# Three weights' splitting moved into the first up projection and kept in DRAM, memory row sums taken from token rows, memory softmax scaling moved to ScalarE

## Chip, cores and metric

The kernel runs on one core of one Trainium2 chip. The metric is the device time of one execution in microseconds (us). Before the change it is 2209.2 us, the median of three runs (2208.19 to 2209.79).

## What is computed

One layer of a decoder trunk over 1024 tokens of width 1024, all in float32:

```
x = x + 1/2 * SwiGLU_1(RMSNorm(x))                 # D_FF = 2816
h = RMSNorm(x); z = h @ W_in                       # [u | v | c_q | c_kv | k_rope | q_mem | gates]
A: u * (tril(W_s) LayerNorm(v) + b)                # 128-token chunks, 8 groups of 64
B: multi-head latent attention, causal, 8 heads
C: cross-attention of q_mem into 256 memory tokens, 4 heads of 128:
   kv = RMSNorm(mem) @ w_kv; k = RMSNorm(k); p = softmax(q k^T / sqrt(128)); p @ v
merged = sum_i sigmoid(gate_i) * (y_i @ W_branch_i)
x = x + merged @ W_out
x = x + 1/2 * SwiGLU_2(RMSNorm(x))
```

The outputs are compared in float32, so each product is made of three matmuls in the faster format fp32r. A number is taken apart into a high part "hi" (its cast to fp32r) and a low part "lo" (what the cast left over), and hi·hi, lo·hi and hi·lo are added.

## The kernel before

**Products and splits.** A product is emitted by a helper whose three matmuls have the lines L147, L148 and L149. A weight, in a load of 512 KB (128 partitions of 1024 numbers), is split by `split`: a cast on ScalarE (ACT, L130) writes `whi`, and a subtraction on VectorE (DVE, L131) writes `wlo`. `split_later` does the same on L135 and L136. The pools decide what may run ahead: `whi` and `wlo` have five tiles each, `raw` three, `w4` eleven, `x4` ten.

**The up projection.** Each feed-forward network is worked off in "units", one for each block f of 128 gate and 128 up columns. A unit makes seven products instead of eight (a Strassen-like scheme), each of 12 matmuls over 512 tokens: 84 matmuls a unit. It needs four pairs of split weights, in this order: "a" (whole 128x1024), "s", "t" (128x1024, sums of loaded halves, made on DVE at L1321) and "l" (128x512). The results of the products are combined on DVE (`add`, L1348), go through a silu on ACT (L1600) and are multiplied by the gate on DVE (L1596). The first product of a unit multiplies by `a`, into the accumulator called `bank`; the last five go into accumulators called `one` or `bank`. Behind each odd f, `spill` subtracts the blocks of two units from each other (on POOL, L1750) and SP stores seven blocks to DRAM (L1757: `tdb` for blocks of the result, `tdt` for their differences).

`up(4)` runs the units f = 4 to 21. In it TensorE's (PE) order is as written in the program. The order on ACT, DVE, POOL and SP (SyncE, which issues nearly all DMAs) is set when the kernel is built, by a scheduler that weighs readiness against the order in the program. On the chip every engine works off its own list strictly in order, and so does SP: an instruction that waits holds all that stand behind it.

**The mixer.** Between the two feed-forward networks stand the input projection, the gates, and the mixer. In the mixer, `sgu` (branch A) loads `w_v` by `load`: pieces of 512 KB into `raw`, each split in halves of 512 columns by L130 and L131 right before the products that use them. `take(0)` and `take(1)` make the v projection of two groups of tokens, `mix` the chunked gating (its u is written by ACT at L662). Beside them the memory side (branch C) goes step by step: `mem_norm` squares the transposed memory on ACT, adds the squares on DVE and sums them over partitions on PE (`token_sums`); `mem_kv` loads the two halves of `w_kv` by `load` and makes keys and values; `mem_attention` makes the softmax: a maximum on DVE (L818), eight exponentials with sums on ACT (L823, 128x256 each) for two tiles, and a multiplication by the reciprocal sums on DVE (L828, 128x1024, eight in all).

## Time and profile before

| what | value |
|---|---|
| median of three runs | 2209.2 us |
| the profiled execution's own time | 2208.74 us |
| its span, first to last instruction | 2206.9 us |
| mean granted TensorE clock in it | 0.996 |
| HBM read / written | 206.00 MB / 86.51 MB |
| up projection, f = 4 to 21 | about 75 to 440 us of the span |
| mixer with memory attention | about 1075 to 1235 us of the span |

The time of an execution is 1.8 us more than its span. Times in the profile are in microseconds from the span's start. A row of the timeline has start, duration, engine, line, operation, output<-inputs and shapes; in brackets how long the engine was idle before it, and what released it. PE's matmuls are pipelined: in full flow one of 128x512 starts every 0.227 us (84 of them make a unit of 19.05 us), though each is shown with 0.39 us. "SPq" is the issue of a DMA by SP; the landing comes later.

### The profile page before, as it was taken

The page shows a single profiled execution, that of the slowest core. Times are in us where ns is not written, and L with a number is a line of the kernel's source. Part 1 is how long each engine was busy: PE and PEld are TensorE (multiplying, and loading weights), DVE is VectorE, ACT ScalarE, POOL GpSimd, SP SyncE. Part 2 cuts the span into 40 slices and gives each one's busy share as a digit, 9 for nine tenths or more (in the row PEclk, how much of TensorE's full clock was granted, in tenths as well). Part 3 has the DMA queues.
Part 4 walks back from the last instruction along what each step waited for, and adds up shares of the span by engine and source line. Part 5 has one row for each costly group of instructions (what it writes and reads, how often), then busy time and mean ns, then how long its engine had stood idle before and what let it go on. Part 6 is the DMA issues. An engine that isn't in the chain of part 4 may idle for free.

```text
span 2206.9 us, 27578 instructions
## 1 busy us (share of the span) xinstructions
PE 2177.5 (99%) x10256; PEld 1816.0 (82%) x10256; DVE 1564.4 (71%) x2402; ACT 912.1 (41%) x1507; POOL 249.4 (11%) x252
## 2 busy tenths in 40 slices
PE   9999999999999999999989999999999999999999
PEld 5788888888887888888878889988888888888887
DVE  7966666579889555544887669885886666657884
ACT  5422222244445333344465449843432222234332
POOL 0012111100000000000400121150011121210000
PEclk9999999999999999999999999999999999999999
DMA  4242323484432333331644740084032333338543
GB/s 144 82 153 91 102 99 110 144 309 157 148 107 93 117 105 124 134 103 39 220 134 148 255 170 30 30 315 181 29 120 97 101 113 100 115 110 300 172 129 105
DMA packets 116085, 294.29 MB, mean 133 GB/s; under 512 B 13680, under 2 KB 22000, under 8 KB 115952
## 3 DMA queue, kind: packets, MB, share of 16 engines
q1 hardware_dynamic: 115952, 292.55, 38.1%
q8 instruction: 80, 1.31, 0.2%
q14 instruction: 53, 0.43, 0.1%
HBM read 206.00 MB, written 86.51 MB: 133 GB/s over the span
## 4 chain that ended last, share of the span: by engine, by line
PE 88%; DVE 7%; ACT 2%; DMA 1%; issue 1%; SPq 0%; POOL 0%; ACTq 0%; DVEq 0%; POOLq 0%
PE one L147 14%; PE one L148 14%; PE one L149 14%; PE bank L147 13%; PE bank L148 12%; PE bank L149 12%; PE mm L147 1%; PE mm L148 1%; PE mm L149 1%; PE bank L948 1%; PE bank L963 1%; PE bank L964 1%; DVE wlo L136 1%; DVE wlo L131 1%; PE bank L425 1%
## 5 line engine op out<-in xcount | busy, mean ns | idle before, releaser
L135 ACT CAST whi<-x 128x1024 fp32r<-128x1024 f32 (+1 forms) x201 | 191.2, 954 | 501.6 <-PE one L148 220.5
L1348 DVE TENSOR_TENSOR t<-t,one 128x512 f32<-128x512 f32 x186 | 127.7, 687 | 244.1 <-PE one L149 243.3
L147 PE MATMUL bank<-h,whi 128*128 128x512 f32 x676 | 263.3, 390 | 0.0
L148 PE MATMUL bank<-h,whi 128*128 128x512 f32 x676 | 263.1, 389 | 0.0
L149 PE MATMUL bank<-h,wlo 128*128 128x512 f32 x676 | 263.0, 389 | 0.0
L136 DVE TENSOR_TENSOR wlo<-x,whi 128x1024 fp32r<-128x1024 f32 (+1 forms) x201 | 239.8, 1195 | 31.7 <-ACT whi L135 31.6
L147 PE MATMUL one<-h,whi 128*128 128x512 f32 x508 | 198.7, 391 | 0.7 <-ACT t L1457 0.7
L149 PE MATMUL one<-h,wlo 128*128 128x512 f32 x508 | 197.7, 389 | 0.0
L148 PE MATMUL one<-h,whi 128*128 128x512 f32 x508 | 197.6, 389 | 0.0
L147 PE MATMUL one<-w,whi 128*128 128x512 f32 x424 | 164.9, 389 | 0.0
L148 PE MATMUL one<-w,whi 128*128 128x512 f32 x424 | 164.9, 389 | 0.0
L149 PE MATMUL one<-w,wlo 128*128 128x512 f32 x424 | 164.9, 389 | 0.0
L130 ACT CAST whi<-w 128x1024 fp32r<-128x1024 f32 (+1 forms) x108 | 95.1, 899 | 144.6 <-PE one L148 62.7
L1750 POOL TENSOR_TENSOR raw<-raw 128x512 f32<-128x512 f32 x38 | 62.9, 1656 | 804.0 <-DVE raw L1596 804.0
L131 DVE TENSOR_TENSOR wlo<-w,whi 128x1024 fp32r<-128x1024 f32 (+1 forms) x108 | 110.2, 1034 | 60.6 <-ACT whi L130 60.5
L149 PEld LDWEIGHTS bank<-h,wlo 128*128 128x128 f32 x676 | 126.9, 188 | 26.3
L148 PEld LDWEIGHTS bank<-h,whi 128*128 128x128 f32 x676 | 126.9, 188 | 26.2
L147 PEld LDWEIGHTS bank<-h,whi 128*128 128x128 f32 x676 | 126.9, 188 | 26.1
L147 PE MATMUL bank<-whi 128*128 128x512 f32 x352 | 136.9, 389 | 0.0
L148 PE MATMUL bank<-wlo,whi 128*128 128x512 f32 x352 | 136.9, 389 | 0.0
L149 PE MATMUL bank<-whi,wlo 128*128 128x512 f32 x352 | 136.9, 389 | 0.0
L147 PEld LDWEIGHTS one<-h,whi 128*128 128x128 f32 x508 | 95.4, 188 | 20.9 <-ACT t L1457 1.1
(398 smaller groups left out, 4893.9 us busy)
## 6 DMA issues: line engine op xcount, KB each, us to landing
x<-in_ffn_w_gu_dram SPq DMA_DIRECT2D x78, 512.0 KB, 4.9
w<-tdt SPq DMA_DIRECT2D x40, 512.0 KB, 4.4
tdb<-raw SPq DMA_DIRECT2D x64, 256.0 KB, 2.1
h<-in_ffn_w_down_dram SPq DMA_DIRECT2D x64, 256.0 KB, 6.0
gate<-raw SPq DMA_DIRECT2D x31, 512.0 KB, 2.6
w<-tdb SPq DMA_DIRECT2D x30, 512.0 KB, 4.6
tdt<-w SPq DMA_DIRECT2D x48, 256.0 KB, 2.0
x<-in_w_gate_dram SPq DMA_DIRECT2D x21, 512.0 KB, 5.6
```

The source lines that it names most:

```text
L130: self.nc.scalar.copy(hi, src)
L131: return (eng or self.nc.vector).tensor_tensor(lo, src, hi.bitcast(F32), op=ALU.subtract)
L135: self.nc.scalar.copy(hi, src)
L136: return lambda: self.nc.vector.tensor_tensor(lo, src, hi.bitcast(F32), op=ALU.subtract)
L147: i = mmul(out, s[0], m[0], start=first, stop=False, **kw)
L148: mmul(out, s[0], m[1], start=False, stop=False, **kw)
L149: self.last = mmul(out, s[1], m[0], start=False, stop=last, **kw)
L425: nc.tensor.transpose(b[:m, k * P:(k + 1) * P], s, self.ident)
L948: nc.tensor.transpose(b[:, at:at + P], prs[t][:, kk * P:(kk + 1) * P], self.ident)
L963: nc.tensor.matmul(o, w, pt[0], start=n == 0, stop=False)
L1348: return self.nc.vector.tensor_tensor(out, x, y, op=ALU.add)
L1750: sub = lambda d, x, y: (eng or nc.gpsimd).tensor_tensor(d, x, y, op=ALU.subtract)
```

## The change

Four edits.

1. A generator `pre_split` is given to `up(4)` as `aside` and takes one step behind each unit from f = 4 on. A step loads 512 KB of `w_v` (four pieces), of the memory keys' weights (four) or of the memory values' weights (four) into a tile of `w4`, splits it by `split`, and stores `whi` and `wlo`, 512 KB each, to DRAM. Twelve units, f = 4 to 15, have such a step. In `sgu` and `mem_kv`, `load_parts` fetches the split pairs straight into `whi` and `wlo`, with no splitting.
2. `mem_norm` gets the sums of squares of the memory's tokens from their rows: two more loads of 512 KB (a new input, the same numbers in another layout, made beforehand like the other layouts), and two squares on ACT that add along the row. The squares of the transposed memory, the additions on DVE and the sum over partitions on PE go.
3. In the softmax of the memory attention, the multiplication by the reciprocal sum is done by ACT, four of 128x256 for each tile, instead of one of 128x1024 on DVE.
4. In `sgu`, the loads of the layer norm's rows go into a tile of `x4`; `next(mem)` moves out of `take(0)`; the memory queries' first step comes behind `mix(1)`'s second, followed by three steps of `branches`; the memory attention's list loses three such steps.

```diff
 
     def __init__(self, ctx, tc, a, out):
         self.tc, self.nc, self.a, self.out, self.last = tc, tc.nc, a, out, None
+        self.parts = {}
         pool = lambda name, bufs=1, **k: ctx.enter_context(tc.tile_pool(name=name, bufs=bufs, **k))
         self.const = pool("const")
         self.small = pool("small", 4)
...
                 self.split(hi[:, c], lo[:, c], raw[:, c], self.nc.gpsimd if at in pool else None)
                 at += 1
             out += [(hi[:, k * width:(k + 1) * width], lo[:, k * width:(k + 1) * width]) for k in range(m)]
+        return out
+
+    def pre_split(self, srcs, room):
+
+        nc = self.nc
+        for key, src in srcs:
+            n, width = src.shape[1:]
+            per = D // width
+            self.parts[key] = parts = [
+                [self.dram.tile([P, D], F32, name=f"pre_{key}_{k}_{x}") for x in "hl"] for k in range(n // per)]
+            for k, part in enumerate(parts):
+                raw = room().rearrange("p a w -> p (a w)")
+                nc.sync.dma_start(raw, src[:, k * per:(k + 1) * per, :].rearrange("p k w -> p (k w)"))
+                hi, lo = self.wide("whi"), self.wide("wlo")
+                self.split(hi, lo, raw)
+                for d, x in zip(part, (hi, lo)):
+                    nc.sync.dma_start(d, x.bitcast(F32))
+                yield
+
+    def load_parts(self, key, width):
+
+        out = []
+        for part in self.parts.pop(key):
+            pair = self.wide("whi"), self.wide("wlo")
+            for x, d in zip(pair, part):
+                self.nc.sync.dma_start(x.bitcast(F32), d)
+            out += [tuple(x[:, k:k + width] for x in pair) for k in range(0, D, width)]
         return out
 
     def mm(self):
...
         nc, a, tc = self.nc, self.a, self.tc
         v8 = lambda tag, dt=F32R: p.tile([P, 4, SGW], dt, name=tag, tag=tag, bufs=2)
         if True:
-            ln_g = self.bcast_row(p, "ln_g", a["sg_ln_g"], SGW)
-            ln_b = self.bcast_row(p, "ln_b", a["sg_ln_b"], SGW)
+            ln = self.x4()
+            ln_g, ln_b = (ln[:, k] for k in range(2))
+            for x, n in ((ln_g, "sg_ln_g"), (ln_b, "sg_ln_b")):
+                nc.sync.dma_start(x, a[n].partition_broadcast(P))
             ws = self.raw().rearrange("p (g t) -> p g t", g=SGG)
             nc.sync.dma_start(ws, a["sg_w"])
             nc.gpsimd.affine_select(
...
             self.split(whi, wlo, ws)
             mem = self.mem_norm()
             next(mem)
-            w = self.load(a["w_v"])
+            w = self.load_parts("v", SGW)
             next(mem)
             vs, yt = [], []
 
...
                     nc.vector.tensor_tensor(u, u, b, op=ALU.mult)
                     self.split(*(t[:, hf * 512:hf * 512 + 512] for t in yt[j]), u)
 
-            take(0, {7: lambda: next(mem)})
+            take(0)
             take(1, {3: lambda: next(mem)})
             m0, m1 = mix(0), mix(1)
             with tc.manual_schedule(engines={mybir.EngineType.PE}):
                 kv = self.mem_kv(next(mem), (lambda: next(m0, None), lambda: next(m0, None)))
                 rooms = [v8(n).rearrange("p (a b) w -> p a (b w)", a=2) for n in ("v_hi", "v_lo")]
                 queries = self.mem_queries([(x[:, 0], x[:, 1]) for x in rooms])
-                next(queries)
                 next(m1)
                 rooms = [v8(n, F32) for n in ("v_hi", "v_lo")]
                 rooms = [x.rearrange("p (a h) (b m) -> p a (h b) m", a=2, b=2)[:, k] for x in rooms for k in range(2)]
                 branch = self.branches(0, yt, sink)
                 next(branch)
                 next(m1, None)
+                next(queries)
+                for _ in range(3):
+                    next(branch)
             yc = self.mem_attention(next(queries), rooms, *kv, branch)
         return yc
 
...
             nc.sync.dma_start(
                 t.rearrange("p a (b m) -> p (a b) m", b=2), a["mem"][:, 4 * n:4 * n + 4])
         yield
-        acc = self.row()[:, :2 * ML].rearrange("p (a m) -> p a m", a=2)
-        for n, t in enumerate(x4):
-            sq = self.x4() if n == 0 else sq2
-            nc.scalar.activation(sq, t, ACT.Square)
-            if n == 0:
-                first, sq2 = sq, self.x4()
-        nc.vector.tensor_tensor(first, first, sq2, op=ALU.add)
-        nc.vector.tensor_tensor(acc, first[:, 0].rearrange("p (a m) -> p a m", a=2),
-                                first[:, 1].rearrange("p (a m) -> p a m", a=2), op=ALU.add)
-        nc.vector.tensor_tensor(acc[:, 0], acc[:, 0], acc[:, 1], op=ALU.add)
+        ss = self.stat("mem_ss", ML // P)
+        sq = self.x4(BF16)
+        for t in range(ML // P):
+            row = self.x4()
+            nc.sync.dma_start(row.rearrange("p a w -> p (a w)"), a["mem_rows"][t])
+            nc.scalar.activation(sq, row, ACT.Square, accum_out=ss[:, t:t + 1])
+        r = self.rms(ss, ML // P, D)
         yield
-        ss = self.token_sums(acc[:, 0], late=True)
-        last = self.final
-        r = self.rms(ss, ML // P, D)
-        yield last
         scale = self.norm_scale(r, late=True, bank=lambda: self.mm()[:, 0])
         last = self.final
         hi, lo = views(2, F32R), views(2, F32R)
...
                     then()
             return ps
 
-        ps = product(self.load(a["mem_w_kv"][0]))
-        w = self.load(a["mem_w_kv"][1])
+        ps = product(self.load_parts("k", MH * MD))
+        w = self.load_parts("vv", MH * MD)
         x = self.h4().rearrange("p a (h d) -> p a h d", h=MH)
         self.head_norm(x, [ps[:, 0], ps[:, 1]])
         amid[0]()
...
                     accum_out=sm[:, hh:hh + 1])
             rs = self.stat("m_rs", MH)
             nc.vector.reciprocal(rs, sm)
-            nc.vector.tensor_tensor(pr, pr, rs.unsqueeze(2).to_broadcast([P, MH, ML]), op=ALU.mult)
+            for hh in range(MH):
+                nc.scalar.activation(pr[:, hh], pr[:, hh], ACT.Copy, scale=rs[:, hh:hh + 1])
             st[i, k] = pr
 
         def turn(i, k):
...
         F = lambda: next(filler, None)
         yt = [self.split_pair(self.h4) for _ in range(MH)]
         for f, *x in (
-                (F,), (F,), (S, 0, 0), (F,), (S, 0, 1), (F,), (T, 0, 0), (S, 1, 0), (F,), (T, 0, 1), (S, 1, 1), (F,),
+                (S, 0, 0), (F,), (S, 0, 1), (F,), (T, 0, 0), (S, 1, 0), (F,), (T, 0, 1), (S, 1, 1), (F,),
                 (V, 0), (T, 1, 0), (S, 2, 0), (F,), (T, 1, 1), (S, 2, 1), (F,), (V, 1), (T, 2, 0), (S, 3, 0), (F,),
                 (T, 2, 1), (S, 3, 1), (F,), (V, 2), (T, 3, 0), (F,), (T, 3, 1), (F,), (V, 3)):
             f(*x)
...
             ffn.start(
                 lambda half, p: from_input(norm.t, half, p),
                 lambda: nc.sync.dma_start(g_ffn1, a["ffn1_norm"]))
-            ffn.up(4)
+            ffn.up(4, self.pre_split(
+                [("v", a["w_v"]), ("k", a["mem_w_kv"][0]), ("vv", a["mem_w_kv"][1])], ffn.w4))
             late = self.late_constants()
             next(late)
             rows = Rows(self)
...
         for n, t in (("b11", b11), ("b21", b21), ("b22", b22), ("t3", t3), ("t1", t1), ("t2", t2), ("t4", t4)):
             nc.sync.dma_start(self.td[n][:, j], t)
 
-    def up(self, first):
+    def up(self, first, aside=iter(())):
 
         with self.k.tc.manual_schedule(engines={mybir.EngineType.PE}):
             for f in range(first, FT):
...
                 self.unit(f)
                 if f % 2 and f < FT - 1:
                     self.spill(f // 2)
+                next(aside, None)
+            for _ in aside:
+                pass
 
 
     def down(self, rows, load, sink, pre={}, post={}, aside=iter(())):
...
     i = {k: np.asarray(v) for k, v in inputs.items()}
     r = {"x": c(i["x"].reshape(S, D).T).reshape(DT, P, S)}
     r["mem"] = c(i["mem"].reshape(ML, DT, P).transpose(2, 1, 0))
+    r["mem_rows"] = c(i["mem"].reshape(ML // P, P, D))
     r["positions"] = c(i["positions"].reshape(NT, P).T)
     r["inv_freq"] = (10000.0 ** (-np.arange(ROPE // 2) / (ROPE // 2))).astype(np.float32)
 
```

Line numbers of the changed kernel are higher by 27 or 28: L130/L131 become L158/L159, L135/L136 become L163/L164, L1304 becomes L1331, L1321 L1348, L1348 L1375, L1367 L1394, L1596 L1623, L1600 L1627, L1757 L1784, and L147 to L149 become L175 to L177.

How the lists of the engines read, at two places of the up projection. In them x_917 or w_1358 is one tile of a pool; a number names one use of it.

ACT before, from the end of unit f = 4 to the first product of f = 6. `x_917` is the last pair (l) of f = 5; `x_1057`, `x_1059`, `x_1060`, `x_1058` are the pairs a, s, t, l of f = 6, and `x_1185` is a of f = 7. The copy `t<-bank` reads the first product of a unit.

```order
L1600 ACTIVATE raw<-bank 128x512
L135 CAST whi<-x_917 128x512
L1600 ACTIVATE t<-t 128x512
L135 CAST whi<-x_1057 128x1024
L1367 COPY t<-bank 128x512
L135 CAST whi<-x_1059 128x1024
L1600 ACTIVATE raw<-bank 128x512
L135 CAST whi<-x_1060 128x1024
L135 CAST whi<-x_1058 128x512
L1600 ACTIVATE t<-t 128x512
L135 CAST whi<-x_1185 128x1024
L1367 COPY t<-bank 128x512
```

So the pair a of a unit is cast one unit ahead: that of f = 6 stands ahead of the copy of f = 5's first product.

ACT after, from the end of unit f = 7 to the first product of f = 8 and on. `w_1358` is the piece of the step behind f = 7, `x_1366`, `x_1368`, `x_1369`, `x_1367` are a, s, t, l of f = 8, `w_1502` is the piece of the step behind f = 8, and `x_1510` is a of f = 9.

```order
L1627 ACTIVATE raw<-bank 128x512
L1627 ACTIVATE t<-t 128x512
L158 CAST whi<-w_1358 128x1024
L163 CAST whi<-x_1366 128x1024
L163 CAST whi<-x_1368 128x1024
L163 CAST whi<-x_1369 128x1024
L163 CAST whi<-x_1367 128x512
L158 CAST whi<-w_1502 128x1024
L1394 COPY t<-bank 128x512
L163 CAST whi<-x_1510 128x1024
```

The piece's cast and behind it the casts of all four pairs of f = 8 now stand behind f = 7's last silu, with no cast of f = 8 ahead of it; the copy of f = 8's first product comes behind them. The same shape stands ahead of f = 5, 6, 10, 12, 14 and 16. The pair a of the odd units from f = 7 on is cast one unit ahead, as before.

DVE after, at the same place. `t<-t,one` reads a product of f = 7, `raw<-raw,t` is its gate.

```order
L1623 TENSOR_TENSOR raw<-raw,t 128x512
L1375 TENSOR_TENSOR t<-t,one 128x512
L1623 TENSOR_TENSOR raw<-raw,t 128x512
L159 TENSOR_TENSOR wlo<-w_1358,whi 128x1024
L164 TENSOR_TENSOR wlo<-x_1366,whi 128x1024
L164 TENSOR_TENSOR wlo<-x_1368,whi 128x1024
L164 TENSOR_TENSOR wlo<-x_1369,whi 128x1024
L164 TENSOR_TENSOR wlo<-x_1367,whi 128x512
L159 TENSOR_TENSOR wlo<-w_1502,whi 128x1024
```

The subtractions of f = 8 have gone behind the piece's, and the piece's behind the last product of f = 7 (its second `t<-t,one` here).

SP after, at the same place. `tdb_1_102` and `tdt_1_103` are stores of the units f = 6 and 7; `x_1510` and `x_1511` are the weights of f = 9.

```order
L1331 DMA x_1510<-in_ffn_w_gu_dram 128x1024
L1331 DMA x_1511<-in_ffn_w_gu_dram 128x1024
L1784 DMA tdt_1_103<-raw 128x512
L1784 DMA tdb_1_102<-raw 128x512
L126 DMA w_1358<-in_w_v_dram 128x1024
L126 DMA w_1502<-in_mem_w_kv_dram 128x1024
L1784 DMA tdt_1_104<-raw 128x512
```

The loads of the two pieces have come in between the stores, behind `tdb_1_102`, which stores what the first of the two gates in DVE's list writes.

## The prediction

> **What bounds the kernel now.** First the page: its head, the busy shares and the chain that ended last.
>
> ```profile
> span 2206.9 us, 27578 instructions
> PE 2177.5 (99%) x10256; PEld 1816.0 (82%) x10256; DVE 1564.4 (71%) x2402; ACT 912.1 (41%) x1507; POOL 249.4 (11%) x252
> PE 88%; DVE 7%; ACT 2%; DMA 1%; issue 1%; SPq 0%; POOL 0%; ACTq 0%; DVEq 0%; POOLq 0%
> ```
>
> TensorE is busy for all but 29.4 of 2206.9 us, so taking work from ACT and DVE cannot in itself be worth much. It can only be worth the waits of PE that it ends, and it costs any wait that it makes. The second view is therefore the waits of PE (line, what it waited for, us in total, times, longest), and the third the windows (length, PE busy with its matmuls, granted clock, DMA share, GB/s).
>
> ```profile
> PE bank L147 <- ACT u L662: 5.0, 1, 5.0
> PE mm L148 <- DVE wlo L131: 2.6, 1, 2.6
> PE bank L147 <- DVE h L140: 2.5, 1, 2.5
> ```
>
> ```profile
> 200.00:300.00 100.00, 100.00 (x443) 1.00 0.31 108
> 300.00:400.00 100.00, 100.00 (x443) 1.00 0.30 102
> 1075.00:1235.00 160.00, 146.99 (x779) 0.95 0.46 155
> ```
>
> The first projection, into which the splitting goes, has no gap: PE is busy for 100.00 of 100.00 us at full clock. The mixer, out of which it comes, has 13.0 us of gaps in 160, the three quoted waits among them, and its clock of 0.95 costs about 160 x 0.05 = 8 us more. **So the mixer can give back some 21 us at the very most, and the up projection has nothing to win and something to lose.** Everything turns on whether PE is still fed there.
>
> **Up projection: the load ahead of the casts.** The lists of ACT, DVE and SP in the section on the change show the step. The piece's load stands on SP right behind `tdb_1_102`; the piece's cast stands on ACT ahead of the pair a of the next unit; its subtraction stands on DVE behind the last gate of the unit that ends. What these instructions take is seen before the change at the end of f = 5 (T = 138.99 is the first matmul of the next unit):
>
> ```profile
> 137.85 0.69 DVE L1596 TENSOR_TENSOR raw<-raw,t 128x512 f32<-128x512 f32 x1
> 138.57 0.33 SPq L1757 DMA_DIRECT2D tdb<-raw  x1
> 138.76 0.39 PE L149 MATMUL one<-x,wlo 128*128 128x512 f32 x1
> 138.99 0.39 PE L147 MATMUL bank<-h,whi 128*128 128x512 f32 x1
> 139.00 1.06 ACT L135 CAST whi<-x 128x1024 fp32r<-128x1024 f32 x1 [1.18 <-PE one L148]
> 139.19 0.69 DVE L1348 TENSOR_TENSOR t<-t,one 128x512 f32<-128x512 f32 x1 [0.64 <-PE one L149]
> 139.91 0.69 DVE L1596 TENSOR_TENSOR raw<-raw,t 128x512 f32<-128x512 f32 x1
> 140.52 2.31 DVE L136 TENSOR_TENSOR wlo<-x,whi 128x1024 fp32r<-128x1024 f32 x1
> ```
>
> PE goes from the last product of f = 5 to the first of f = 6 with no gap, since that unit's pair a had been split a unit ahead. The store `tdb` is held until the first gate (137.85) ends; it leaves at 138.57, 0.42 us before T. Behind it SP can issue the piece's load at about T - 0.05; what two such issues and their landing take, two other answers say (loads of the same 512 KB, the first pair issued behind `tdb` at 160.1, then all of the stage):
>
> ```profile
> 159.67 0.33 SPq L1757 DMA_DIRECT2D tdb<-raw  x1
> 160.09 0.87 SPq L1304 DMA_DIRECT2D x<-in_ffn_w_gu_dram  x2
> DMA to landing us min/median/max: 4.0/4.5/4.9
> DMA to landing us min/median/max: 4.0/4.9/5.6
> ```
>
> So the piece lands at T + 4.0 to T + 4.9, and ACT stands still on its cast until then. The prices behind it, and one row of DVE's shortest run of the subtraction:
>
> ```profile
> L135 ACT CAST whi<-x 128x1024 fp32r<-128x1024 f32 x44 | 46.4, 1054 | 103.4 <-DVE x L1321 61.8 <-PE one L148 16.6 <-issue 15.6
> 159.56 1.22 DVE L136 TENSOR_TENSOR wlo<-x,whi 128x1024 fp32r<-128x1024 f32 x1
> ```
>
> Cast of the piece 1.05, cast of a 1.05: PE's first matmul (it needs a's `whi`) starts at T + 6.1 to 7.0. DVE subtracts the piece from the end of its cast (T + 5.0 to 5.9) in 1.22, then a in 1.22: the third matmul, the first that needs `wlo`, starts at T + 7.5 to 8.4. Without the wait it starts at T + 0.45. **The stall is 7.0 to 7.9 us; I take 7.5.** Behind it nothing is late: the next pair (s) is split 1.05 and 1.22 us after a, and the first product has 12 matmuls of 0.227 us, 2.7 us. DVE's list also shows what is queued behind: the combining of the next unit's products, which needs those products first.
>
> How often: the shape stands ahead of f = 6, 8, 10, 12, 14 and 16, so 6 x 7.5 = 45. The odd units from 7 on keep their pair a a unit ahead, and the second piece of a pair of units is cast in the middle of a unit, where ACT has 19 us for under 7 us of work (three casts of 1.05 and short ones of 0.6): nothing. The 24 stores of split pairs stand on SP behind that cast and ahead of the weights of the next unit but one, which are not due for another 19 us: nothing either. Ahead of f = 5 the load stands behind earlier stores:
>
> ```profile
> 116.70 0.95 SPq L1757 DMA_DIRECT2D tdb<-w  x2
> ```
>
> They leave by 117.65, T is 119.9 (138.99 - 19.05), the load lands at 121.7 to 122.6, and the third matmul starts 3.5 later, at 125.2 to 126.1 instead of 120.4. Were the load one issue earlier the stall would be about 4, so I take 4.7 from 4 to 5.7. **Stalls together: 50 us, from 46 to 53.**
>
> **Up projection: the clock after the stalls.** The trace of before has gaps of this kind in the mixer. Windows of 5 us around them, and one beside a gap that cost nothing more:
>
> ```profile
> 1080.00:1085.00 5.00, 2.44 (x11) 1.00 0.79 261
> 1135.00:1140.00 5.00, 0.07 (x1) 0.69 0.75 243
> 1140.00:1145.00 5.00, 5.00 (x21) 0.63 0.74 285
> 1155.00:1160.00 5.00, 2.59 (x19) 1.00 0.53 157
> 1160.00:1165.00 5.00, 4.86 (x24) 0.66 0.20 71
> ```
>
> The gap of 5.0 us lies in 1135 to 1140, and behind it the clock stays low: 0.63 in the next 5 us. The gap of 2.5 us (1157.6 to 1160.1) brings 0.66, the gap of 2.6 us (before 1083.8) keeps 1.00. Two gaps of one length with different outcomes: it depends on where a gap falls on a fixed grid, and gaps of 2.5 us can be enough. The sum of clock lost in the rows behind the gaps, 5 x 0.37 = 1.85 and 5 x 0.34 = 1.7 us, is what I take for each stall: 1.7 us, from 0.85 to 2.6 (a gap of 6 us always fills more than half a step of such a grid). Seven stalls: **12 us, from 6 to 18.**
>
> [...]
>
> **Mixer.** The splitting that goes, and DVE's and ACT's share of the softmax scaling:
>
> ```profile
> L131 DVE TENSOR_TENSOR wlo<-raw,whi 128x512 fp32r<-128x512 f32 x28 | 19.8, 720 | 0.5 <-ACT whi L130 0.5
> L828 DVE TENSOR_TENSOR v_hi<-v_hi,m_rs 128x1024 f32<-128x1024 f32 x4 | 4.9, 1225 | 0.1
> L823 ACT ACTIVATE v_lo<-mm,m_mx,mq_nr 128x256 f32<-128x256 f32 x16 | 8.9, 576 | 5.3 <-DVE m_mx L819 5.3
> raw<-in_mem_w_kv_dram SPq DMA_DIRECT2D x8, 512.0 KB, 4.2
> ```
>
> DVE loses 24 subtractions of 0.72 (17 us) and 8 scalings of 1.225 (9.8 us), ACT loses 24 casts and gains 32 scalings (each at most the 0.58 us of an exponential of that shape, 18 us). The work moved is beside PE, so it counts by the three waits only. The wait of 2.6 us for a split `wlo` goes: its pair is loaded. The wait of 5.0 us for u gets shorter, as the layer norm's rows come earlier and DVE has less ahead of it; I give it 2.3. Two matmuls of PE (`token_sums`) go: 0.5. Against it: the row loads, the two squares and the memory's scaling now stand closer to the keys' product, and the twelve pieces now come as 24 loads of 512 KB instead of 12, each at 4.2 us to landing; I reckon with a new wait of about 3 us for the memory side. With clock unchanged: 2.6 + 2.3 + 0.5 - 3 = **2.4, rounded to a gain of 3 us**. Ends: a gain of 14 (both waits, their clock, and no new wait) and a loss of 10 (two waits of 5 us, as the one above, for loads of twice the bytes). PE in this stage is all but full, so these ends are far apart on purpose.
>
> **Rivals.**
>
> *The loads are there in time (B).* If SP got the pieces out well before T, the piece's load would hold nobody. What stays is DVE's list: product 139.19, gate 139.91, then the piece's and a's subtractions, 140.52 + 1.22 + 1.22 = 142.96, T + 3.97 instead of T + 0.45. Stall 3.5 x 7 = 24.5, clock 7 x 1.4 = 10, mixer -3: 2208.7 + 31.5 = 2240. Against it: SP's list has the load behind `tdb_1_102`. [...]
>
> *Stalls are longer (D).* Two piece loads leave together with the stores of the spill; at 5.6 us to landing each stall gets 1 us longer, and if a low clock lasts through two steps of the grid, as behind the 5.0 us gap (0.69, then 0.63), each costs 3.4 instead of 1.7. 6 + 12 more: 2285.
>
> *Not slower (C).* PE isn't held at the start of a unit because the pair a is split in time; then only the mixer counts. It decides at the landing: a piece that lands by T - 3.5 (issued by T - 8) and a subtraction ahead of the last gates. Price 0 in the up projection, mixer -3 to -21: 2188 to 2206, say 2197. For it: ACT is busy for only 41%, DVE for 71%, there is room for the twelve splits in 360 us (12 x 1.05 and 12 x 1.22). Against it: the order in which the lists hold them, which the chip can't change. Even rival B's 24.5 us would outweigh the mixer's greatest gain.
>
> **How the numbers follow.** The profiled execution took 2208.74 us, 1.8 more than its span and 0.5 less than the median 2209.2; sums stand on 2208.7. Forecast: 2208.7 + 50 + 12 - 3 = 2267.7, of which I name **2267** (chance 0.65; its own bounds 2208.7 + 46 + 6 - 14 = 2247 and 2208.7 + 53 + 18 + 10 = 2290). B: 2240 (0.12). D: 2285 (0.17). C: 2197 (0.06), of which 0.01 within 0.2%. The range 2238 to 2288 takes in B's value and D's, and leaves out C, B's low clock and the far ends, about 2 in 10. A measurement of this kernel can tell about 0.2%, 4.4 us, from no change. Faster 0.05, same 0.01, slower 0.94.
>
> **What would show it.** Right: seven new entries in PE's waits at the first product of a unit (`bank`, now L175 and L177) for ACT's `whi` and DVE's `wlo` of the weights, about 6 us and 1 us each, at about 120, 145, 193, 240, 287, 335 and 382 us of the span (19.05 us a unit, plus about 9 us for each stall before); the piece's cast L158 idle until its load; windows there at about half clock behind each stall; the first projection some 60 us longer, everything behind it shifted; the mixer's gaps near 13 us still. Wrong: a piece issued by SP a unit ahead (B or C), PE waits of under 4 us there (B), low clock for 7 us at a time (D), or a mixer whose gaps have changed by more than 10 us.

## The result and the profile after

The changed kernel takes 2277.8 us (median of four runs, 2276.0 to 2279.9), the kernel before 2209.2 us in the same session: ratio 1.031, 95% interval 1.029 to 1.033. It is 3.1% slower. The forecast was 2267 with a range of 2238 to 2288. The profiled execution of after took 2275.99 us, its span is 2274.3 us.

The page of after: head, busy shares, and the shares of the chain that ended last.

```profile
span 2274.3 us, 27622 instructions
PE 2195.2 (97%) x10252; PEld 1822.4 (80%) x10252; DVE 1544.0 (68%) x2379; ACT 922.4 (41%) x1529; POOL 237.6 (10%) x252
PE 84%; DVE 4%; ACT 4%; DMA 2%; issue 1%; SPq 0%; ACTq 0%; DVEq 0%
```

TensorE (PE) is idle for 79 us instead of 29, and is shown busy for 18 us longer with the same matmuls; most of the second number is the lower clock (below). The waits of PE (line, what it waited for, us in total, times, longest):

```profile
PE bank L175 <- ACT whi L163: 45.2, 8, 7.4
PE bank L175 <- ACT u L692: 5.4, 4, 2.5
PE bank L177 <- DVE wlo L164: 3.2, 7, 1.8
PE bank L175 <- DVE wlo L159: 2.7, 2, 2.0
PE mm L177 <- DVE h L159: 2.1, 1, 2.1
```

The first and the third row are new and stand in the first projection: seven stalls, at 120.7, 147.8, 195.4, 242.7, 290.8, 338.5 and 386.6 us, which are the first products of f = 5, 6, 8, 10, 12, 14 and 16. (The eighth wait of the first row is 0.2 us in the second network.) One of them in full, the start of f = 8 and the second shortest of the seven, from the timeline of after:

```profile
194.16 0.69 DVE L1623 TENSOR_TENSOR raw<-raw,t 128x512 f32<-128x512 f32 x1 [0.76 <-ACT t L1627]
194.88 0.33 SPq L1784 DMA_DIRECT2D tdb<-raw  x1
195.00 0.39 PE L177 MATMUL one<-x,wlo 128*128 128x512 f32 x1
195.25 0.42 SPq L126 DMA_DIRECT2D w<-in_w_v_dram  x1
199.68 1.04 ACT L158 CAST whi<-w 128x1024 fp32r<-128x1024 f32 x1 [5.56 <-DMA w<-in_w_v_dram]
200.63 3.45 ACT L163 CAST whi<-x 128x1024 fp32r<-128x1024 f32 x4
200.76 1.22 DVE L159 TENSOR_TENSOR wlo<-w,whi 128x1024 fp32r<-128x1024 f32 x1 [3.92 <-ACT whi L158]
201.73 0.80 PE L175 MATMUL bank<-h,whi 128*128 128x512 f32 x1 [6.34 <-ACT whi L163]
201.90 4.09 DVE L164 TENSOR_TENSOR wlo<-x,whi 128x1024 fp32r<-128x1024 f32 x4
202.32 0.63 PE L176 MATMUL bank<-h,whi 128*128 128x512 f32 x1
203.17 0.79 PE L177 MATMUL bank<-h,wlo 128*128 128x512 f32 x1 [0.23 <-DVE wlo L164]
```

Read it down the left column. The gate writes its block until 194.85; the store that waited for it leaves at 194.88; behind it SP issues the piece's load at 195.25; ACT has stood still for 5.6 us when the piece has landed, casts it (199.68) and only then the pair a of f = 8 (200.63); PE's first matmul starts at 201.73 instead of at 195.23 (T, the unit's start without a wait), its third at 203.17. At f = 10, 12, 14 and 16 the piece lands later. The longest stall is f = 14, where T is 338.38 and the load leaves at 338.40:

```profile
343.89 1.04 ACT L158 CAST whi<-w 128x1024 fp32r<-128x1024 f32 x1 [6.62 <-DMA w<-in_mem_w_kv_dram]
347.38 0.80 PE L177 MATMUL bank<-h,wlo 128*128 128x512 f32 x1 [0.23 <-DVE wlo L164]
```

Measured as the prediction measures a stall, by how late the third matmul starts, the seven lie between 5.6 us (f = 5) and 8.6 us (f = 14), 54.1 us together. The windows (length, PE busy, granted clock, DMA share, GB/s) show the second part of the price:

```profile
195.00:199.80 4.80, 0.39 (x2) 1.00 0.79 232
199.80:206.60 6.80, 4.65 (x10) 0.50 0.87 337
206.70:212.00 5.30, 5.30 (x25) 1.00 0.84 258
```

From 199.8 to 206.7 the granted clock is half, and PE is back at work from 201.7: 4.65 us of work at half speed, 2.3 us lost. Of the 6.8 us of low clock, 3.5 lie behind the third matmul, at 203.17.

To see where the 67.3 us between the spans lie, the spans are cut at waits of PE that every kernel here has: the wait for DVE's t at 70.0 us (before) and the one at 685.0; PE's wait ahead of the latent products at 1035.8; and the wait for the attention's first maximum at 1298.3. Lengths between them:

| stage | before | after | difference |
|---|---|---|---|
| start | 70.0 | 70.8 | +0.8 |
| first network (up and down) | 614.95 | 680.78 | +65.8 |
| gates and input projection | 350.85 | 350.80 | -0.1 |
| mixer up to the causal attention | 262.52 | 263.66 | +1.1 |
| the rest | 908.62 | 908.26 | -0.4 |

### The profile page after: what moved, and what is told of

It reads as the page before. It is cut to its first block, busy times and chain, and to the rows that moved or that the text cites. A ratio compares the mean times of both kernels' runs of the same rounds, so it can differ in the third digit from the quotient of the medians.

```text
span 2274.3 us, 27622 instructions
## 1 busy us (share of the span) xinstructions
PE 2195.2 (97%) x10252; PEld 1822.4 (80%) x10252; DVE 1544.0 (68%) x2379; ACT 922.4 (41%) x1529; POOL 237.6 (10%) x252
## 4 chain that ended last, share of the span: by engine, by line
PE 84%; DVE 4%; ACT 4%; DMA 2%; issue 1%; SPq 0%; ACTq 0%; DVEq 0%
PE one L175 13%; PE one L177 13%; PE one L176 13%; PE bank L177 12%; PE bank L175 12%; PE bank L176 12%; PE mm L175 2%; PE mm L177 2%; PE mm L176 2%; PE bank L974 1%; DMA w<-in_mem_w_kv_dram 1%; PE bank L989 1%; DVE wlo L164 1%; PE bank L990 1%; ACT whi L158 1%
## 5 line engine op out<-in xcount | busy, mean ns | idle before, releaser
L163 ACT CAST whi<-x 128x1024 fp32r<-128x1024 f32 (+1 forms) x201 | 188.8, 952 | 406.1 <-PE one L176 179.8
L175 PE MATMUL bank<-h,whi 128*128 128x512 f32 x676 | 269.7, 399 | 44.9 <-ACT whi L163 44.9
L1375 DVE TENSOR_TENSOR t<-t,one 128x512 f32<-128x512 f32 x186 | 127.6, 686 | 261.8 <-PE one L177 261.1
L177 PE MATMUL bank<-h,wlo 128*128 128x512 f32 x676 | 268.8, 398 | 3.2 <-DVE wlo L164 3.2
L176 PE MATMUL bank<-h,whi 128*128 128x512 f32 x676 | 268.2, 397 | 0.0
L164 DVE TENSOR_TENSOR wlo<-x,whi 128x1024 fp32r<-128x1024 f32 (+1 forms) x201 | 232.4, 1167 | 30.0 <-ACT whi L163 26.2
L175 PE MATMUL one<-h,whi 128*128 128x512 f32 x508 | 198.7, 391 | 0.7 <-ACT t L1484 0.7
L177 PE MATMUL one<-h,wlo 128*128 128x512 f32 x508 | 197.7, 389 | 0.0
L175 PEld LDWEIGHTS bank<-h,whi 128*128 128x128 f32 x676 | 130.2, 193 | 74.2 <-ACT whi L163 47.9
L159 DVE TENSOR_TENSOR wlo<-w,whi 128x1024 fp32r<-128x1024 f32 (+1 forms) x120 | 124.8, 1053 | 89.9 <-ACT whi L158 89.0
L158 ACT CAST whi<-w 128x1024 fp32r<-128x1024 f32 (+1 forms) x120 | 107.6, 913 | 187.3 <-PE one L176 62.7
L175 PE MATMUL one<-w,whi 128*128 128x512 f32 x424 | 165.4, 390 | 0.0
L177 PE MATMUL one<-w,wlo 128*128 128x512 f32 x424 | 165.0, 389 | 0.0
L177 PEld LDWEIGHTS bank<-h,wlo 128*128 128x128 f32 x676 | 129.7, 192 | 34.8 <-DVE wlo L164 7.9
L176 PEld LDWEIGHTS bank<-h,whi 128*128 128x128 f32 x676 | 130.1, 192 | 27.0
L177 PE MATMUL bank<-whi,wlo 128*128 128x512 f32 x352 | 137.0, 389 | 0.0
L175 PE MATMUL bank<-whi 128*128 128x512 f32 x352 | 137.0, 389 | 0.0
L175 PEld LDWEIGHTS one<-h,whi 128*128 128x128 f32 x508 | 95.4, 188 | 20.8 <-ACT t L1484 1.1
```

Of the source, the lines that this page charges most:

```text
L158: self.nc.scalar.copy(hi, src)
L159: return (eng or self.nc.vector).tensor_tensor(lo, src, hi.bitcast(F32), op=ALU.subtract)
L163: self.nc.scalar.copy(hi, src)
L164: return lambda: self.nc.vector.tensor_tensor(lo, src, hi.bitcast(F32), op=ALU.subtract)
L175: i = mmul(out, s[0], m[0], start=first, stop=False, **kw)
L176: mmul(out, s[0], m[1], start=False, stop=False, **kw)
```

## Experiments

Theory: PE waits at seven unit starts because the piece's load is issued at the end of a unit and everything that the next unit needs stands behind the piece's cast. Rivals: the lost splitting ahead of the pair a alone does it, whatever the load does; the 13 us of casts, 15 of subtractions and 19 MB of traffic (twelve loads and 24 stores of 512 KB) that came into the projection cost PE by themselves; or the other three edits carry part of the loss. The table gives every run, with the stages cut as above (the low step of the clock near 72 us, told of at the end, adds about 1 us to the first network in some of the profiles).

| kernel | us (median) | ratio to before, 95% | first network | mixer |
|---|---|---|---|---|
| before | 2209.4 to 2210.0 | | 614.95 | 262.52 |
| changed | 2277.8 | 1.0293 to 1.0329 | 680.78 | 263.66 |
| e1 split one unit later | 2216.0 | 1.0019 to 1.0040 | 620.30 | 263.92 |
| e2 pair a ahead, load late | 2263.6 | 1.0229 to 1.0259 | 665.28 | 265.92 |
| e3 splitting alone | 2276.5 | 1.0286 to 1.0316 | 681.88 | 262.83 |
| e4 other edits alone | 2214.0 | 1.0009 to 1.0028 | 615.81 | 267.46 |
| e5 inside the unit | 2211.5 | 0.9999 to 1.0019 | 615.00 | 263.13 |
| e6 as e1, scaling on DVE | 2212.8 | 1.0002 to 1.0021 | 620.27 | 260.86 |
| e7 as e1, sums on PE | 2217.9 | 1.0021 to 1.0047 | 619.19 | 266.64 |
| e8 as e1, norm rows late | 2208.8 | 0.9989 to 1.0007 | 620.11 | 259.12 |
| e9 as e5, norm rows late | 2205.6 | 0.9971 to 0.9989 | 615.93 | 257.53 |
| e10 as e9, scaling on DVE | 2203.9 | 0.9959 to 0.9983 | 615.48 | 256.89 |
| e11 as e10, order of before | 2208.4 | 0.9985 to 1.0003 | 615.05 | 261.08 |
| e12 as e5, splitting alone | 2212.0 | 1.0000 to 1.0018 | 616.28 | 263.60 |

The stages are those of one profiled execution each. The changed kernel, e1, e2 and e5 have the same mixer in the program, and it takes 263.1 to 265.9 us in them, with other waits (e2 has one of 1.8 us for ACT's exponentials that the changed kernel has not). A difference of less than 3 us between two mixers is therefore no proof for an edit by itself.

### e1: the same loads, used one unit later

`fetch` takes a tile for the next piece and issues its load, as `pre_split` did.

```diff
+        ready = [fetch()]
+        yield
+        while ready[0]:
+            ready.append(fetch())
+            part, raw = ready.pop(0)
             hi, lo = self.wide("whi"), self.wide("wlo")
             self.split(hi, lo, raw)
```

> All of the change, but each piece is split and stored one step after its load was issued (the first step only loads). The loads stay at their places in SP's list, with the same bytes, casts, subtractions and stores. Theory (PE waits because the piece's load is issued at the unit's end and everything for the next unit stands behind its cast): no stall at a unit's start, first projection back to its time of before, 2277.8 - 65.7 = 2212 us, from 2208 to 2216. Rival (12 MB more of traffic or 12 more splits on ACT and DVE cost PE time by themselves): at least a third of the 65.7 us stays, 2234 us or more.

Measured: 2216.0 us, at the edge of what the theory gave and far from the rival's. The seven stalls are gone, though bytes, casts, subtractions and stores are the same and the loads leave at the same places. The window of e1 over the projection:

```profile
80.00:460.00 380.00, 377.55 (x1658) 1.00 0.50 170
```

And all of PE's waits in it:

```profile
PE one L187 <- DVE t L1387: 2.3, 4, 1.0
```

The DMA share is 0.50, where the windows of before had 0.30 and 0.31, and PE is idle for 2.45 of 380 us, at full clock. So 60 of the 65.8 us came from the piece landing too late for its place in the lists. About 5 us stay: four waits for DVE's combining, the low step near 72 us of about 1 us, and matmuls that start late by less than the view shows as idle.

### e2: the pair a ahead of the piece, the load still late

```diff
+                if f < FT - 1:
+                    if f + 1 not in self.quad:
+                        self.fetch(f + 1)
+                    self.sums(f + 1)
+                    self.made[f + 1] = self.weights(f + 1, "a")
                 next(aside, None)
```

> All of the change, but the pair a of the next unit is split ahead of the piece; the piece's load stays behind the store at the unit's end, and the pair s of the next unit now stands behind the piece. Theory (the load's landing sets the wait, whichever pair stands behind it): the first product runs, then PE waits at the second product, at about 2.7 us from the unit's start, until s is split at about 8.0: 4.9 us of stall seven times and 1.7 us of clock each, 46 us over 2212, so 2258 us, from 2245 to 2266. Rival (only the place of the pair a matters, as the split ahead was lost): no stall, 2212 us. Rival (traffic or split work): about 2278 us as before.

Measured: 2263.6 us, as the theory had it (2258, from 2245 to 2266). PE runs the first product, and waits at the second one. ACT and PE at the start of f = 8 (T = 189.3 here), from the timeline:

```profile
193.96 1.04 ACT L158 CAST whi<-w 128x1024 fp32r<-128x1024 f32 x1 [1.06 <-DMA w<-in_w_v_dram]
194.91 2.51 ACT L163 CAST whi<-x 128x1024 fp32r<-128x1024 f32 x3
196.01 0.79 PE L175 MATMUL one<-w,whi 128*128 128x512 f32 x1 [3.78 <-ACT whi L163]
197.46 0.79 PE L177 MATMUL one<-w,wlo 128*128 128x512 f32 x1 [0.23 <-DVE wlo L164]
```

And all of PE's waits in the projection:

```profile
PE one L175 <- ACT whi L163: 26.2, 7, 4.8
PE one L177 <- DVE wlo L164: 3.9, 7, 1.8
```

The waiting product is now `one<-w` instead of `bank<-h`, and its third matmul starts at T + 8.1 (forecast 8.0): the stall moved from the pair a to whichever pair stands behind the piece, and shrank by what the first product covers. The rival that blamed the place of the pair a alone (2212 us) falls.

### e3 and e4: the parts of the change by themselves

e3 has `mem_norm`, `sgu`'s order and norm rows, and `mem_attention` with its scaling as before the change, and takes its weights by `load_parts`. The seven stalls are in e3 as they were:

```profile
PE bank L175 <- ACT whi L163: 45.9, 8, 7.8
```

e4 is the opposite:

```diff
-            w = self.load_parts("v", SGW)
+            w = self.load(a["w_v"])
...
-            ffn.up(4, self.pre_split(
-                [("v", a["w_v"]), ("k", a["mem_w_kv"][0]), ("vv", a["mem_w_kv"][1])], ffn.w4))
+            ffn.up(4)
```

> Only the splitting in the first projection and the loading of the parts; the memory sums, the softmax scaling, the layer norm rows and the mixer's order are as in the kernel before. Theory: the first projection is again 65.7 us longer with seven stalls, and the mixer alone changes: without the 24 splits its two waits for wlo (2.6) and u (5.0) are shorter, 2209.2 + 65.7 - 4 = 2271 us, from 2266 to 2278. Rival (the other three edits carry part of the loss): 2260 us or less.

> Without the splitting in the first projection: the three weights are loaded and split in the mixer as before; memory sums from rows, scaling on ACT and the new order stay. Theory: the first projection is as before (no stall), only the mixer changes; with the splits back on ACT and DVE and the scaling on ACT besides, its waits grow by a few us: 2213 us, from 2207 to 2220. Rival (the other three edits carry part of the loss of 68 us): 2220 us or more.

Measured: 2276.5 and 2214.0 us. The splitting alone has the whole loss of the first network (+66.9, a low step near 72 us among it). Its mixer did not get shorter, though, against the 4 us that I expected: +0.3 us. The other edits alone make the mixer 4.9 us longer, and nothing else.

### e5: the split inside the unit

On top of e1; `next(steps)` emits the first product:

```diff
-                self.unit(f)
+                steps = self.unit_steps(f)
+                next(steps)
+                next(aside, None)
+                for _ in steps:
+                    pass
                 if f % 2 and f < FT - 1:
                     self.spill(f // 2)
-                next(aside, None)
```

> All of the change, with each piece's split one step behind its load (as in the run with 2216.0 us) and taken behind the first product of a unit instead of at its end. In ACT's and DVE's lists the split then stands in the middle of a unit. Theory: the 2.3 us in which the run with 2216.0 us still waited for DVE's combining at L1387 (a piece's subtraction ahead of it) shrink to under 0.5; mixer unchanged: 2214 us, from 2210 to 2217. Rival (traffic or split work in the first projection costs by itself): 2216 us or more.

Measured: 2211.5 us. The first network takes 615.00 us against 614.95 before: the twelve splits cost it nothing. The window of e5 over the projection:

```profile
80.00:420.00 340.00, 340.00 (x1500) 1.00 0.50 166
```

PE is busy for 340 of 340 us at a DMA share of 0.50. That settles both what was left of e1 (subtractions at a place where DVE's combining waited for them) and the rival of traffic and work.

### e6, e7, e8: the mixer's edits undone, one by one, in e1

> As the run with 2216.0 us (pieces split one unit later), but the softmax scaling is back on DVE, 128x1024 at once. Theory (this work lies beside PE): within 2 us of 2216. Rival (the 32 short scalings of ACT hold what PE waits for in the memory attention): 2213 us or less, with shorter waits there.

> As the run with 2216.0 us, but the memory's sums of squares come again from the transposed memory, with additions on DVE and a sum over partitions on PE, at their place of before. Theory (the new wait of 2.1 us ahead of the keys' product comes from the row loads and the scaling behind them): that wait goes, and 0.5 us of PE comes back: 2214 us, from 2211 to 2217. Rival (the wait comes from the shorter way to the keys' product, not from the rows): 2216 us or more.

> As the run with 2216.0 us, but the layer norm's rows are loaded into their own tiles, as before the change. Theory (their early load shortened the wait for u from 5.0 to 2.6 us): the wait for u is about 5 us again, with its low clock, 2218 us, from 2215 to 2221. Rival (the splits that left the mixer shortened it): no difference, 2214 to 2217 us.

e6, with one multiplication of 128x1024 on DVE again: 2212.8 us, the mixer 3.1 us shorter. I had expected no difference; the rival was right. Where e1 has waits for DVE's maximum and combining at 1219 to 1227 us (0.65, 0.34 and 0.43), e6 has none. These are 1.4 of the 3.1 us; the 95% intervals of e1 and e6 just overlap.

e7, with the sums on PE again: 2217.9 us, the mixer 2.7 us longer, against an expected gain. The intervals of e1 and e7 overlap, so this run alone would not show a loss; e12 below does it again. The wait ahead of the keys' product did go. Another came, at the start of the v product:

```profile
PE mm L187 <- ACT v L564: 3.3, 1, 3.3
```

ACT there, from the timeline of e7:

```profile
1083.29 0.87 ACT L552 ACTIVATE sq<-bank 128x384 f32<-128x384 f32 x2 [4.96 <-DVE qk_ss L565]
1085.14 1.06 ACT L765 ACTIVATE x<-x 128x1024 f32<-128x1024 f32 x1 [0.98 <-DMA x<-in_mem_dram]
1086.11 0.58 ACT L562 ACTIVATE sq<-mm 128x512 f32<-128x512 f32 x1
1086.59 0.58 ACT L563 COPY k<-mm 128x512 f32<-128x512 f32 x1
1087.05 0.60 ACT L564 COPY v<-mm 128x512 f32<-128x512 f32 x1
```

The square of the transposed memory (L765) waits for its load, and the copies that give PE its accumulator back stand behind it.

e8, with the layer norm's rows in tiles of their own and loaded late: 2208.8 us. It was expected to lose 2 us, and it gained 7: the mixer is 4.8 us shorter (the two profiled executions differ by 5.2 us, the medians by 7.2). The two longest waits for u are 1.60 and 3.06 us, and the 2.1 us ahead of the keys' product are gone. The reason is in another place than I looked: in the loads of the memory's rows. First SP and ACT in e1, then in e8:

```profile
1102.93 3.75 SPq L590 DMA_DIRECT2D qd<-q  x2
1106.73 2.22 SPq L766 DMA_DIRECT2D x<-in_mem_rows_dram  x1
...
1114.37 1.06 ACT L767 ACTIVATE x<-x 128x1024 bf16<-128x1024 f32 x1 [3.15 <-DMA x<-in_mem_rows_dram]
```

```profile
1098.08 2.33 SPq L764 DMA_DIRECT2D x<-in_mem_rows_dram  x1
...
1110.11 1.05 ACT L765 ACTIVATE x<-x 128x1024 bf16<-128x1024 f32 x1
```

In e1 the second row tile's load is issued 8.7 us later, its square ends at 1115.4 instead of 1111.2, and the memory's scaling on DVE (L449) starts at 1122.4 instead of 1119.4. SP did not stand still for a tile there: from 1099.6 us on it issues with no break of over 0.4 us, and the load goes out as soon as the two stores of `qd` ahead of it are issued. What shows is the load's place in SP's list: counted from a store of `vd` near 1075 us, 28 DMAs stand ahead of it in e1 and 22 in e8. Undoing the edit moved it forward. Whether the tile that the norm's rows borrow from `x4`, the pool of the memory's rows too, put it so far back when the kernel was built, or the two loads that the edit puts at the head of SP's list, no run keeps apart.

### e9 to e12: towards a version that beats both

> Pieces split inside the unit (2211.5 us) and the layer norm's rows in their own tiles, loaded late as before the change. Theory (both gains add: the first projection has no wait left, and the second memory row's load gets its tile of the pool early, so the keys' product doesn't wait): 2211.5 - 4.8 = 2206.7 us, from 2204 to 2210. Rival (the gain of late rows came with the other splitting place only): 2211 us.

> As the run before, and the softmax scaling back on DVE. Theory (ACT's 32 short scalings stretch the memory attention by about 3 us whatever stands ahead): 2203.7 us, from 2201 to 2207. Rival (it is hidden here, or DVE becomes the one waited for): 2206 us or more.

> As the run before, and the queries and the three steps of the branches at their places of before the change. Theory (with the queries' product later, nothing covers the second group's wait for u of some 3 us; at its old place it does): 2 us less than the run before, 2202 us, from 2199 to 2205. Rival (the new order is what the splits' removal needs): 2 us more or worse.

> Only the splitting in the first projection, inside the units and one step behind its loads; the rest of the mixer as before the change. Theory (the first projection hides the whole of it, and the mixer gains little, as in the run with the splitting alone, whose mixer was 0.3 us longer): 2209.5 us, from 2206 to 2213, no difference from before. Rival (24 splits fewer in the mixer are worth their waits): 2204 us or less.

e9 came out at 2205.6 us, the two gains added. e10, with the scaling on DVE besides, at 2203.9: ratio 0.9971, interval 0.9959 to 0.9983, which is 0.3% below the kernel before and the lowest median of all runs. Its interval and that of e9 overlap, and the mixers differ by 0.6 us only, so the 3 us of e6 did not come a second time. The waits of e10 in the mixer:

```profile
PE bank L187 <- ACT u L702: 5.0, 3, 3.1
PE bank L187 <- DVE h L180: 1.1, 1, 1.1
PE mm L187 <- DVE a_mx L961: 1.0, 1, 1.0
PE bank L187 <- DVE t L1057: 0.9, 1, 0.9
PE mm L187 <- DMA whi<-pre_v_h: 0.8, 1, 0.8
```

e11 shows that the new order is worth something: with the order of before the mixer is 4.2 us longer, and the wait for u is one of 5.3 us again, so my expectation had the wrong sign.

```profile
PE bank L187 <- ACT u L702: 6.0, 2, 5.3
PE bank L187 <- DVE h L180: 2.6, 1, 2.6
```

e12, the splitting alone at its good place, is no faster than before (2212.0 us; the mixer +1.1). By themselves 24 splits fewer in the mixer bring nothing here; with the other three edits in place the mixer is 3.8 us shorter without them (the changed kernel against e4). e12 differs from e11 only by the sums of the memory on PE instead of from rows (and the place that this gives one step of `mem_norm`), and is slower by 3.6 us, its mixer by 2.5: that is what e7 showed.

## Why the prediction was right, step by step

**Where and how the stalls come.** Right at every step. Seven stalls, at the seven unit starts that the lists gave. At f = 8, with T = 195.23 (forecast in brackets): the store leaves at T - 0.35 (T - 0.42), the load at T + 0.02 (T - 0.05), it has landed at T + 4.45 (4.0 to 4.9), PE's first matmul starts at T + 6.5 (6.1 to 7.0), its third at T + 7.9 (7.5 to 8.4). e1 and e2 show the cause: the same loads used a unit later take the stalls away, and another pair behind the late piece takes over the wait.

**Size of the stalls.** Too small by 4 us: 54.1 against 50, and just outside the 46 to 53. At f = 5, 6 and 8 the third matmul is 5.6, 7.8 and 7.5 us late, inside the bounds (4 to 5.7 for f = 5, 7.0 to 7.9 for the others). At f = 10, 12, 14 and 16 it is 8.1 to 8.6 us late. There the piece landed at T + 5.0 to T + 5.5, where I had taken T + 4.0 to T + 4.9 from loads of before. The twelve pieces took this long from issue to landing:

```profile
DMA to landing us min/median/max: 4.4/5.4/6.4
```

PE's idle time in the waits, 45.0 + 3.2 = 48 us, is less than 54 because two matmuls run before the third and are shown as busy.

**The clock.** Right in size: 12 us forecast, from 6 to 18, and 65.8 - 54.1 = 11.7 us measured. The low time that is left behind each stall's third matmul, 22.9 us in all at half speed, gives 11.5. But each low stretch lasted 6.83 us, two steps of 3.41, where my price stood for one (for two I had put 3.4 us a stall, in the rival of longer stalls); in all seven, part of the first step passed while PE still waited, so it cost less than its length. My 1.7 us was read from the rows behind two gaps in the mixer. In the trace of before the clock is low for 6.83 us from 1136.87 on, of which 3.70 lie in the first of these rows, and for 3.41 us from 1160.76 on, all in the second: such a remainder, and one whole step. The number held, but in part by luck. That a gap fills more than half a step, as I put it beside the 1.7, is not enough for a low clock here: 1.75 us without work in a step of 3.41 brought none in e5 (last section).

**The mixer.** Forecast a gain of 3 us, measured a loss of 1.1. The wait for `wlo` (2.6) went, the first group's wait for u shrank from 5.0 to 2.3 us, and a new one of 2.1 us came ahead of the keys' product, as the sum had it. What it lacked were small new ones: the second group's wait for u (2.5 and 0.6), a DMA of the parts (1.0), a split of 2.0 at the end of the memory attention. The gaps of the stage sum to 14.0 us instead of 13.2. By the experiments, the early norm rows lose (4.8 us in e1, 5.6 in e5) and so, less surely, does the scaling on ACT (3.1 us in e1, 0.6 in e9); the rows for the sums and the new order gain (2.5 to 2.7 and 4.2). I had judged the scaling as work beside PE; in e6 waits of PE went with it, in e10 it was worth 0.6 us only.

**The sum.** The profiled execution took 2276.0 us, 8 more than the sum's 2267.7: 4.1 for the stalls, 4.1 for the mixer, and 0.3 less for the clock against 0.3 more for all the rest. Its median is 1.8 us above it.

**The rivals.** Longer stalls (2285) is nearer to the measured 2277.8 than the 2267 that I named, by 7 us against 11, and both its conditions came true in part: pieces that landed later at four of the seven starts, and a low clock of 7 us at a time, which I had listed as a sign against my forecast. Its price for that clock, 3.4 us a stall, did not come. Loads in time (2240) did not happen; e1 shows how it would have been, at 2216, better than I put it, since with the loads in time the pair a goes ahead again. (The 1.4 us of clock for each stall in its sum was my estimate; no run shows it.) Not slower (2197) needed that list and a better mixer: e10 is that case, at 2203.9.

## What to carry to other kernels

A prefetch that is issued and used in the same step is none: ACT was busy for 41% of the span here, and yet its seven waits for a piece "on the side", 39.7 us together, held the casts of the next unit behind them in its list. Issue its load a step earlier (here +66 us became +5) and put its use where the neighbours have slack (0). A time to landing measured before a change need not hold after it: the median of these loads was 5.4 us, where 4.9 had been measured in the same stage. And look up what a moved load does to the others in the queue's list: here two small loads sent early went with a later load of the memory's rows, and the kernel lost by it.

## What the runs showed of the hardware

Before the end of the program the granted clock fell from 1.00 to 0.50 for 3.41 or 6.83 us at a time in the traces of before and after, and after each of the seven stalls of over 5 us it stayed low for 6.83 us, two steps of 3.41. In the changed kernel's trace it fell at 124.75, 152.05, 199.84, 247.63, 295.41, 343.20 and 390.99 us: 8 steps apart, then 14 each time. The falls in its mixer, at 1189.71, 1227.25 and 1251.15 us, come 234, 11 and 7 steps later. In the trace of before the falls at 1136.87, 1160.76 and 1174.41 us are 7 and 4 steps apart. So in both traces the falls lie on a fixed grid of 3.41 us, the grid that the prediction speaks of.

A gap of 2.1 us near 70 us of the span, the same in all kernels, brought a low step in seven of the fourteen profiles (beginning at 70.9 to 72.7 us, 3.41 us long) and none in the others: where the gap falls on the grid differs from execution to execution. Laid over the grid that the other falls of each trace's clock record give, the two groups part without exception. In the seven with a low step the gap lies whole inside one step of the grid, and the clock falls at that step's end; in the other seven an edge cuts the gap, and the larger part is 1.1 to 1.75 us (1.50 in before, 1.47 in after). e6 and e5, one window for each step of the grid:

```profile
67.50:70.90 3.40, 1.35 (x7) 1.00 0.00 0
70.90:74.30 3.40, 3.40 (x9) 0.50 0.00 0
```

```profile
67.20:70.60 3.40, 1.65 (x8) 1.00 0.01 2
70.60:74.00 3.40, 3.08 (x14) 1.00 0.00 0
```

PE is idle for 2.05 us of the first step in e6, and for 1.75 in e5. The prediction's two gaps of one length, 2.51 and 2.56 us, come out the same way: the first lies whole in one step, from 1157.35 to 1160.76, where the clock falls; the second is cut at 1082.25 into 1.0 and 1.5 us. With the low step the first network took about 0.9 us longer (615.81 in e4, whose projection is that of before, against 614.95). That is part of the 0.1 to 0.2% by which executions of one kernel differ (2207.6 to 2212.3 us in 28 runs of the kernel before).

Once in each of the fourteen profiles the clock fell with no gap: in the mixer's 32 matmuls with an output of 128x2 (4.2 us of them before, from 1171.5; low from 1174.4), or within 1.2 us behind them. The profile shows PE busy there; why the clock fell is open.

Matmuls in plain float32 (L1649, 128x512) started every 0.429 us in the trace of before, from 24.3 to 37.6 us at a clock of 1.00; those of fp32r start every 0.227 us.
